# First layer: modulation blocks beside the heads, three instructions on three engines or one on VectorE

## The chip, the cores and the metric

The kernel runs on 1 core of one Trainium2 chip. The metric is the device time of one execution in microseconds (us), here the median of 3 runs. The engines are called as in the profile: PE (TensorE; PEld are its weight loads), DVE (VectorE), ACT (ScalarE), POOL (GpSimd), and SP, which does no arithmetic here and issues most of the transfers.

## The reference, cut to what matters

The network has two blocks on 512 tokens of width 1024; the change touches the first layer of the first block. Each layer of that block is modulated by vectors made from one conditioning vector `c`:

```python
c_act = jax.nn.silu(c)
mod = c_act @ w_ada[layer] + b_ada[layer]
shift, scale, gate = mod[:, :D], mod[:, D:2 * D], mod[:, 2 * D:]
h = _modulated_norm(x, norm_g[layer], shift, scale)
y = _gdn_mixer(h, ...)                       # first layer: 8 heads of a gated delta rule
x = x + gate[:, None, :] * y
```

The second layer needs its own `mod` and `mkv = c_act @ w_ada_kv + b_ada_kv`. In all these are 64 blocks of 128 outputs, and each is a product of a 128 x 1024 weight block with one vector of 1024, plus a bias.

## The kernel before, in words

A modulation block is made without PE. `ada` (lines 181 to 195) issues a 512 KB load of the weight block on SP's queue into a tile `ada` (line 187), and returns a function that does the arithmetic. With `off=False` that is one DVE instruction (line 189): it multiplies the tile with the vector `c_rep`, sums along the row and adds the bias, into one column of `mods`. With `off=True` it is three: the product on POOL (line 192), a copy with a running sum on ACT (line 193), and the addition of the bias, 128 x 1, on DVE (line 194).

The first 16 blocks (shift and scale of the first layer) are made at the start, on DVE, since nothing can be projected before them (`OFF` is empty). The other 48 are wanted later: the gate of the first layer in its output projection (line 346), the rest at the start of the second layer (lines 781 and 782). They stand in the list `late`, and are made beside the heads, from a pool of 2 buffers (line 394).

The eight heads come next. `project(h)` computes a head's four 128-column blocks of the input projection (`proj_T`): SP loads a weight block `wr`, ACT writes its rounded part `wh` (line 115), POOL in most cases the remainder `wl` (line 118), and PE runs three matmuls (lines 122 to 124). `conv` follows on ACT and DVE (lines 488 to 493). `gdn_head` has two long chains of small steps:
- the inverse of a triangular matrix in five levels (lines 651 to 670): POOL makes a masked copy `Lm` (line 653), PE and ACT alternate (lines 657 to 667), and DVE subtracts to give the next X (line 669);
- the scan over eight chunks (lines 686 to 702): PE (line 692), DVE (`u`, line 693), PE (line 696), DVE (state `S`, line 701), in turn.

At the end of a head DVE writes its output `oT` (line 717). A planner orders each engine's instructions ahead of time, so that one head's scan, the next head's inverse and the projection of the one after run side by side; each engine then works through its own list in order. What the planner may not do is put an instruction ahead of one it is tied to.

`aside(ins)` (line 513) is called six times in each head: behind the five X updates (line 669) and behind `oT` (line 717). Each call takes the oldest waiting block of the list `came`, issues its arithmetic with `tc.issue_after(ins.ins)`, and asks for the load of the next block (line 522). `issue_after` ties to `ins` only instructions on the engine of `ins`, which is DVE. In the kernel before, the DVE instruction of a block is the addition of the bias alone, so the product on POOL and the sum on ACT are free to run earlier. `came` starts with two blocks that are made with `off=False` (line 509), the 46 others have `off=True`. There are 48 calls, so all 48 blocks are taken by them, and the loop behind the heads (lines 537 to 542) finds nothing left.

After the heads, `residual` (line 561) projects `oT` with `w_out_a` in two parts: the first seven heads' share first, then the eighth's. Its input is split into `oH` on ACT (line 115) and `oL` on DVE (line 118).

Of the kernel before, what the change touches and what calls it, by code (L numbers as in the profile page):

```python
# [372 lines left out]
class Gdn(Net):  # L373
# [9 lines left out]
    def gdn(self):  # L383
# [5 lines left out]
        with ExitStack() as st:  # L389
# [4 lines left out]
            ap = st.enter_context(tc.tile_pool(name="g_ada", bufs=2))  # L394
# [101 lines left out]
            def silu_z(cb, p):  # L496
# [7 lines left out]
            late = [(w_, j0 + j, bias[:, j:j + 1], o[:, j:j + 1]) for w_, j0, n, bias, o in (  # L504
                (a["w_ada"][0], 16, 8, self.col("b_ada", 16, 8), self.mod0[:, 16:24]),
                (a["w_ada_kv"], 0, 16, self.col("b_ada_kv"), self.modk),
                (a["w_ada"][1], 0, 24, self.col("b_ada", 24, 24), self.mod1)) for j in range(n)]

            came = [self.ada(ap, *late.pop(0)) for _ in range(2)]
# [3 lines left out]
            def aside(ins):  # L513
                owed[0] += self.RATE
                if owed[0] < 1:
                    return
                owed[0] -= 1
                if came:
                    with tc.issue_after(ins.ins):
                        came.pop(0)()  # L520
                if late:
                    came.append(self.ada(ap, *late.pop(0), True))
            self.aside = aside

            def project(h):
# [12 lines left out]
            while late or came:  # L538
                if came:
                    came.pop(0)()  # L540
                if late:
                    came.append(self.ada(ap, *late.pop(0), len(late) % self.LV != 0))
            oH = hp.tile([P, KC, T], F32R, tag="hH", name="oH")
            oL = hp.tile([P, KC, T], F32R, tag="hL", name="oL")
            for k in range(KC):
# [1194 lines left out]
```

## Time and profile before

| what | us |
|---|---|
| median of 3 runs | 2809.49 |
| lowest and highest of them | 2806.31 and 2812.97 |
| the profiled execution, its own time | 2804.78 |
| its span, first to last instruction | 2803.0 |
| PE busy in the span | 2630.9 |
| POOL busy in the span | 1743.7 |
| DVE busy in the span | 1696.8 |
| ACT busy in the span | 1208.7 |

Times in the rows are us from the start of the span. The profiled execution lies 4.7 us below the median of the runs. Of the span, the first 110 us are the start and the first head's projection, 110 to 430 most of the work of the heads, and 430 to 510 the rest: the scan of the last two heads beside the output projection. A busy PE need not be PE at its peak, because matmuls are pipelined.

### The profile page before, as it was taken

Reading aid. Unit: us, or ns where it says so; the run is one execution under the profiler, and the core shown is the slowest. Engines: PE = TensorE matmul, PEld = TensorE weight load, DVE = VectorE, ACT = ScalarE, POOL = GpSimd, SP = SyncE. Lnnn points to the kernel's source line nnn. Section 1 sums busy time; section 2 is a strip of 40 time slices with the busy share of each in tenths; the row PEclk is TensorE's granted clock in tenths of the full one; section 3 lists DMA queues with packets and bytes.
Section 4 is the critical chain, followed back from the end, with each engine's and each line's share of the span. In section 5 each row is a group of like instructions: output and inputs, shape, how many; then the busy total and the mean of one; then the engine's idle time right before and its main releaser. Section 6 shows DMA issues by size and latency. Waiting matters only on the chain. (4 is left out here: it accounts for less than half of the span.)

```text
span 2803.0 us, 40405 instructions
## 1 busy us (share of the span) xinstructions
PE 2630.9 (94%) x14601; PEld 2246.9 (80%) x14601; DVE 1696.8 (61%) x3082; ACT 1208.7 (43%) x2505; POOL 1743.7 (62%) x1348
## 2 busy tenths in 40 slices
PE   6999998799997689999998999999999999999998
PEld 4887777697776577787777899999999977877776
DVE  7767663614446456222232597798776167678887
ACT  5676653636664344333333333344434333333332
POOL 4899873543232333444365368878788478887886
PEclk9999999899998799999999999999999999999999
DMA  6343331221011011222122378888888889999996
GB/s 241 106 142 122 116 103 32 77 92 61 29 42 50 31 55 52 78 73 76 65 72 97 124 262 298 311 292 314 312 296 312 280 286 333 344 331 334 334 325 227
DMA packets 206794, 499.35 MB, mean 178 GB/s; under 512 B 18305, under 2 KB 106625, under 8 KB 203521
## 3 DMA queue, kind: packets, MB, share of 16 engines
q1 hardware_dynamic: 167856, 359.19, 38.1%
q0 software_dynamic: 36864, 134.23, 13.4%
q10 hardware_dynamic: 1872, 3.33, 0.4%
q8 instruction: 115, 1.88, 0.3%
q14 instruction: 87, 0.70, 0.1%
HBM read 444.26 MB, written 52.43 MB: 177 GB/s over the span
## 5 line engine op out<-in xcount | busy, mean ns | idle before, releaser
L118 POOL TENSOR_TENSOR wl<-wr,wh 128x256 fp32r<-128x256 f32 (+2 forms) x513 | 425.3, 848 | 466.3 <-ACT wh L115 430.6
L118 POOL TENSOR_TENSOR upl<-upr,uph 128x1024 fp32r<-128x1024 f32 x128 | 311.9, 2437 | 96.5 <-ACT uph L115 95.5
L115 ACT ACTIVATE wh<-wr 128x256 fp32r<-128x256 f32 (+2 forms) x556 | 228.0, 445 | 326.4 <-PE pj L123 113.4
L122 PE MATMUL pj<-nH,downh 128*128 128x384 f32 x1024 | 352.5, 344 | 2.4 <-ACT w L1559 1.3
L124 PE MATMUL pj<-nH,downl 128*128 128x384 f32 x1024 | 348.9, 341 | 2.5 <-DVE downl L118 2.5
L123 PE MATMUL pj<-nL,downh 128*128 128x384 f32 x1024 | 348.9, 341 | 0.0
L118 POOL TENSOR_TENSOR downl<-downr,downh 128x1024 fp32r<-128x1024 f32 x96 | 238.2, 2483 | 131.0 <-ACT downh L115 129.8
L1604 PE MATMUL acc<-uph,wwh 128*128 128x512 f32 x768 | 301.6, 398 | 8.1 <-ACT wwh L115 8.1
L1604 PE MATMUL acc<-upl,wwh 128*128 128x512 f32 x768 | 305.2, 398 | 0.0
L115 ACT ACTIVATE downh<-downr 128x1024 fp32r<-128x1024 f32 x128 | 135.4, 1059 | 309.9 <-PE pj L123 191.6
L118 DVE TENSOR_TENSOR wwl<-wo,wwh 128x384 fp32r<-128x384 f32 x128 | 215.2, 1683 | 63.0 <-ACT wwh L115 59.8
L1604 PE MATMUL acc<-uph,wwl 128*128 128x512 f32 x768 | 232.2, 398 | 6.5 <-DVE wwl L118 6.4
L122 PE MATMUL pj<-hH,wh 128*128 128x512 f32 x544 | 224.5, 413 | 1.7 <-ACT mv L1290 0.7
L124 PE MATMUL pj<-hH,wl 128*128 128x512 f32 x544 | 221.2, 408 | 0.9 <-POOL wl L118 0.8
L123 PE MATMUL pj<-hL,wh 128*128 128x512 f32 x544 | 216.3, 398 | 0.0
L115 ACT ACTIVATE uph<-upr 128x1024 fp32r<-128x1024 f32 x128 | 134.8, 1053 | 174.9 <-POOL upl L118 122.8
L122 PEld LDWEIGHTS pj<-nH,downh 128*128 128x128 f32 x1024 | 193.0, 189 | 5.4 <-ACT downh L115 1.6
L124 PEld LDWEIGHTS pj<-nH,downl 128*128 128x128 f32 x1024 | 193.1, 189 | 3.7 <-DVE downl L118 3.5
L123 PEld LDWEIGHTS pj<-nL,downh 128*128 128x128 f32 x1024 | 193.1, 189 | 0.3
L1604 PEld LDWEIGHTS acc<-uph,wwh 128*128 128x128 f32 x768 | 144.7, 188 | 46.4 <-ACT wwh L115 11.6
L1604 PEld LDWEIGHTS acc<-uph,wwl 128*128 128x128 f32 x768 | 144.9, 189 | 43.8 <-DVE wwl L118 8.7
L1604 PEld LDWEIGHTS acc<-upl,wwh 128*128 128x128 f32 x768 | 145.1, 189 | 34.9
(627 smaller groups left out, 6549.8 us busy)
## 6 DMA issues: line engine op xcount, KB each, us to landing
downr<-in_peer_down_j SPq DMA_DIRECT2D x128, 512.0 KB, 4.8
upr<-in_peer_up_j SPq DMA_DIRECT2D x128, 512.0 KB, 5.7
wr<-in_w_in SPq DMA_DIRECT2D x50, 512.0 KB, 4.2
ada<-in_w_ada SPq DMA_DIRECT2D x48, 512.0 KB, 3.7
wait<-w SPq DMA_DIRECT2D x128, 192.0 KB, 4.9
wo<-wait SPq DMA_DIRECT2D x128, 192.0 KB, 4.9
G<-stage SPq DMA_DIRECT2D x24, 1024.0 KB, 7.3
Gt<-G SPq DMA_DIRECT2D x48, 512.0 KB, 7.9
```

The lines of the kernel that those rows point to most:

```text
L115: nc.scalar.activation(h, src, AF.Copy)
L118: return (eb or nc.vector).tensor_tensor(l, src, h.bitcast(F32), op=ALU.subtract)
L122: mm(out, lh, rh, start=start, stop=False)
L123: mm(out, lh, rl, start=False, stop=False)
L124: mm(out, ll, rh, start=False, stop=stop)
L1604: mm(po[z][b], lh[:, zs], rh[:, bs], start=False, stop=j == P - 1 and rh is uh and lh is l, skip_group_check=True)
```

## The change

Every block made beside the heads takes the form with one DVE instruction. The second edit makes the same choice in the loop behind the heads.

```diff
--- before.py
+++ after.py
@@ -519,7 +519,7 @@
                     with tc.issue_after(ins.ins):
                         came.pop(0)()
                 if late:
-                    came.append(self.ada(ap, *late.pop(0), True))
+                    came.append(self.ada(ap, *late.pop(0)))
             self.aside = aside
 
             def project(h):
@@ -539,7 +539,7 @@
                 if came:
                     came.pop(0)()
                 if late:
-                    came.append(self.ada(ap, *late.pop(0), len(late) % self.LV != 0))
+                    came.append(self.ada(ap, *late.pop(0)))
             oH = hp.tile([P, KC, T], F32R, tag="hH", name="oH")
             oL = hp.tile([P, KC, T], F32R, tag="hL", name="oL")
             for k in range(KC):
```

## Rows read from the trace of the kernel before

**Rows 1.** Busy time by stretch: start:end and length, then each engine, clock, DMA share, GB/s.
```profile
60.00:110.00 50.00, 49.44 (x258) 39.46 (x258) 40.80 (x70) 35.04 (x92) 33.91 (x39) 1.00 0.26 79
110.00:430.00 320.00, 299.07 (x1863) 254.17 (x1862) 221.32 (x401) 204.28 (x526) 286.05 (x241) 0.99 0.37 119
```
**Rows 2.** Groups by line, 110 to 430 us: busy us, mean ns, idle before.
```profile
L192 POOL TENSOR_TENSOR ada<-ada,c_rep 128x1024 f32<-128x1024 f32 x46 | 111.2, 2417 | 4.6 <-DMA ada<-in_w_ada 3.7 <-PE pj L124 0.5 <-DMA ada<-in_w_ada_kv 0.2
...
L193 ACT ACTIVATE ada<-ada 128x1024 f32<-128x1024 f32 x46 | 48.5, 1054 | 5.5 <-POOL ada L192 5.4
...
L194 DVE TENSOR_TENSOR mods<-mods,cols 128x1 f32<-128x1 f32 x40 | 31.8, 798 | 0.0
```
**Rows 3.** Tiles ada and mods: ns min/median/max, first and last start.
```profile
L192 POOL TENSOR_TENSOR ada<-ada,c_rep x46: 2336/2376/3083, 111.5 to 389.8; 128x1024 f32<-128x1024 f32 x46
...
L189 DVE CUSTOM_DVE_ANT_0 ada<-ada,c_rep,cols x18: 1268/1275/2414, 17.4 to 122.4; 128x1024 f32<-128x1024 f32 x18
...
L194 DVE TENSOR_TENSOR mods<-mods,cols x46: 141/369/4648, 137.2 to 499.4; 128x1 f32<-128x1 f32 x46
L189 DVE DVE_READ_ACCUMULATOR2_ANT mods<- x18: 72/76/82, 19.6 to 123.9; 128x1 f32 x18
...
L189 DVE CUSTOM_DVE_ANT_0 ada<-ada,c_rep,cols x1: 1534/1534/1534, 122.4 to 122.4; 128x1024 f32<-128x1024 f32 x1
```
**Rows 4.** Timeline near 233 us: start, us, instruction, idle before and its releaser.
```profile
232.83 2.39 POOL L192 TENSOR_TENSOR ada<-ada,c_rep 128x1024 f32<-128x1024 f32 x1
...
233.06 4.65 DVE L194 TENSOR_TENSOR mods<-mods,cols 128x1 f32<-128x1 f32 x1
...
238.37 0.33 PE L588 MATMUL n<-c_id,y 128*128 128x128 f32 x1 [0.85 <-DVE vb L637]
```
**Rows 5.** Timeline near 132, 292 and 382 us.
```profile
131.63 2.34 POOL L192 TENSOR_TENSOR ada<-ada,c_rep 128x1024 f32<-128x1024 f32 x1
...
131.94 2.05 DVE L594 TENSOR_TENSOR cols<-gcol,cols 128x8 f32<-128x8 f32 x1
...
134.04 0.65 PE L146 MATMUL n<-c_id,cols 128*128 128x128 f32 x4 [2.25 <-DVE cols L594]
...
291.30 3.06 DVE L711 TENSOR_TENSOR ss<-ss,cols 128x4 f32<-128x4 f32 x2
...
294.49 0.49 PE L569 MATMUL n<-rr,selr 128*128 128x512 f32 x1 [3.40 <-DVE rv_q L138]
...
382.18 2.24 DVE L594 TENSOR_TENSOR cols<-gcol,cols 128x8 f32<-128x8 f32 x1
...
385.94 0.80 PE L692 MATMUL s<-S,WQ 128*128 128x128 f32 x2 [2.57 <-DVE S L701]
```
**Rows 6.** What PE waited for, 110 to 430 us: total us, times, longest.
```profile
PE s L692 <- DVE S L701: 4.0, 4, 2.6
...
PE v L657 <- DVE Xv L669: 2.3, 5, 0.8
```
**Rows 7.** Timeline of DVE in the tail, 433 to 501 us.
```profile
433.21 0.35 DVE L701 SCALAR_TENSOR_TENSOR S<-S,gl,s 128x128 f32<-128x128 f32 x1 [0.63 <-PE s L696]
...
447.52 0.34 DVE L701 SCALAR_TENSOR_TENSOR S<-S,gl,s 128x128 f32<-128x128 f32 x1
...
500.18 0.69 DVE L118 TENSOR_TENSOR oL<-oT,oH 128x512 fp32r<-128x512 f32 x1 [0.63 <-ACT oH L115]
```
**Rows 8.** What SP waited for, 110 to 430 us: total us, times, longest.
```profile
SPq L187 <- ACT ada L193: 169.6, 34, 12.0
SPq L262 <- POOL wl L118: 50.4, 11, 16.5
```
**Rows 9.** The page: loads of the blocks (KB each, median us to landing).
```profile
ada<-in_w_ada SPq DMA_DIRECT2D x48, 512.0 KB, 3.7
```
**Rows 10.** Timeline of DVE near 150 us: three additions close together.
```profile
149.25 1.36 DVE L194 TENSOR_TENSOR mods<-mods,cols 128x1 f32<-128x1 f32 x2
...
151.13 0.70 DVE L194 TENSOR_TENSOR mods<-mods,cols 128x1 f32<-128x1 f32 x1
```

## The prediction

> **What bounds the kernel now.** The change lies in the stretch of the heads, so I looked at the busy times by stretch first [rows 1]. From 110 to 430 us PE is busy 299.1 of 320 us (93%), against 49.4 of 50 (99%) in the 50 us before, where no block is made beside the work. So PE sets the pace of the heads, and at most some 20 us of idle PE are to be had there. POOL is busy 286 us (89%) and DVE 221 (69%). Behind 430 us the scans of the last heads set the end. Next, the groups by line [rows 2]: the blocks take 111.2 us of POOL, its largest item, 48.5 of ACT and, for 40 additions of one column, 31.8 of DVE. An addition that can take 0.14 us takes 0.80 on average, and once 4.65 [rows 3]. The timeline says why [rows 4]: the long one starts 0.23 us behind a product of 2.39 us on POOL, and outlasts it. Others with both inputs in SBUF show the same: one of 128 x 8 takes 2.05 us beside a product that starts 0.31 us earlier and ends with it, and PE waits 2.25 us behind it [rows 5]. So the blocks cost PE little by their own work and something by what they hold up on DVE.
>
> **The change, part by part.** The sum is made on the profiled execution, 2804.78 us (span 2803.0), which is 4.7 us under the median of the runs.
>
> The second edit issues nothing: 48 calls take all 48 blocks, so the loop behind the heads is empty. Cost 0.
>
> POOL loses 46 products, 111.2 us, and ACT 46 copies, 48.5 us. Neither bounds the stretch, so that time as such is worth nothing; what counts is what waited for it. Four waits of PE can be read [rows 4, 5]. At 134.04 PE waited 2.25 us for an instruction that the product covers from 131.94 to 133.97: 2.0 back. At 385.94 it waited 2.57 us behind the same instruction of another head, stretched to 2.24: 2.1 back. At 294.49 it waited 3.40 us behind a pair stretched to 3.06; a pair can also stand behind POOL's other work, so I count two thirds, 2.2. At 238.37 the 4.65 us addition itself made 0.85. That is **-7.2 us**. The bounds: 0, if the planner puts other late work in those places, and -17.6, which is what 320 us would give up if PE were busy 99% as in the 50 us before (299.1/0.989 = 302.4).
>
> DVE gets 46 instructions of the long form. The trace has 18 at 1.27 us and up to 2.41 in the worst case; the only one beside the heads took 1.53, to which 0.08 for reading the sum comes [rows 3]. I take 1.61, because that one met the same neighbours. Of the 46, 40 lie before 430 us: 40 x (1.61 - 0.80) = 32.4 us more on DVE. What stands behind them is each time an X update or a state S of the other head. PE now waits 4.0 us for S and 2.3 for X [rows 6], 6.3 us beside 31.8 us of additions, or 0.20 of them. Passed on at that rate, 32.4 us make **+6.4 us**. The bounds are 0 and 32.4.
>
> The order changes too. Today the product runs as soon as POOL is free: the first starts at 111.5 us and its addition at 137.2, the last at 389.8 and its addition at 499.4 [rows 3]. Afterwards the whole work of a block is tied to the X update or `oT`. Six additions stand behind 430 us (46 less 40), and their whole blocks thus move into the tail, where POOL's part is long done. There the scan of the seventh head runs beside the last inverse, and four of its S stand right behind an addition [rows 7]: two with some 0.6 us of idle DVE between (0.63 at 433.21), two with none (447.52). With 1.35 in place of 0.15 us they come 0.6, 0.6, 1.2 and 1.2 us later, 3.6 us. PE reaches its next step late in some of these, so I take half, **+1.8 us**, bounds 0 and 3.6. The last block stands behind `oT` of the eighth head at 499.40, and delays `oL` at 500.18 [rows 7] by 1.2 - 0.6 = **+0.6 us**; nothing else is left for PE there.
>
> The transfers: no load is added, but the buffer of a block now comes free when its DVE instruction ends, and the load of the block after next waits for that. Product and sum had freed it earlier. Such a load lands 3.7 us after its issue [rows 9], so from one addition to the next but one 1.35 + 3.7 = 5.1 us are needed, and 46 additions over 362 us [rows 3] leave 15.7 on average. Close together they are near 150 us, three within 1.9 us [rows 10]. There DVE would stand 3.2 us, with X and S behind it; half of that is **+1.7 us**, bounds 0 and 3.2. SP, where the loads queue with the weights, is treated as a rival.
>
> Sum: -7.2 + 6.4 + 1.8 + 0.6 + 1.7 = +3.3 us, so 2808.1 on the profiled execution, **2812.8 us** on the median. A measurement of this kernel tells about 0.2% from no change, 5.6 us.
>
> The trace shows DVE held by POOL [rows 4, 5]; whether a DVE instruction also holds POOL no row here shows by itself. The Trainium skill, "SBUF — State Buffer", section "Who interferes with whom", says that a DVE instruction with two SBUF inputs and a GpSimd instruction that reads SBUF exclude each other, and that whoever issues first keeps the port for its whole length. By that rule the new instruction, whose tile and vector both lie in SBUF, holds up POOL in turn, and the time would be that of the third rival below.
>
> **The rivals.**
> 1. *Freed engines win (faster).* POOL falls to 175 of 320 us and ACT by a quarter, so masked copies, weight remainders and copies out of PSUM come when PE wants them, and the planner hides the DVE work behind projection matmuls. For: DVE has 99 us of idle time there, and POOL is close to full. Against: in the trace PE hardly waits for POOL itself. With PE at 99% and the tail as above: -17.6 + 2.4 = -15.2 us, 2794.3.
> 2. *DVE stands before a load (slower).* SP issues in order and stands for its buffers: 169.6 us before block loads and 50.4 before weight loads, there up to 16.5 us at a time [rows 8]. Today a late block load is POOL's matter. Afterwards the DVE instruction waits for it at the head of DVE's list, with X, S and the convolution behind it, so PE follows. It decides once SP holds a block load longer than the 15.7 - 5.1 = 10.6 us that an average pair leaves. If a quarter of 46, 12, wait 2 us each and PE loses all of it, that is +24; with 7.2 given back and 2.4 in the tail +19.2, or 2828.7.
> 3. *POOL is held (slower).* If each of 40 instructions holds POOL half its time, 0.68 us, that is 27 us, at 0.20 another +5.4: 2818.2. Against: POOL has 111 us more room.
> 4. *Nothing measurable depends on it*: all of it hides, 2809.5.
>
> **How the numbers follow.** Chances: forecast 0.42, freed engines 0.28, DVE before a load 0.22, POOL held 0.05, nothing 0.03. The forecast's own range is 2806 to 2820: its terms are sized by a rate taken from few waits, and the planner's new order adds a few us either way. Of its 0.42, 0.29 end within 5.6 us, 0.11 above, 0.02 below. Faster: 0.26 of freed engines and 0.02, 0.28. Slower: 0.11 + 0.21 + 0.05 = 0.37. The same: 0.35. The range over all cases is 2794 to 2831: it reaches to the two outer ones, and leaves out more gain than theirs and a longer standing of DVE.
>
> **What would show it.** In the profile after, POOL's busy time from 110 to 430 should be near 175 us and DVE's at most 254 (221 + 32.4), less what its other instructions no longer stand behind POOL. The 128 x 8 instruction should be back below 0.5 us on average, and PE's wait for it gone. PE's waits for S and X should rise from 6.3 to 10 to 15 us. If DVE has idle time that ends with a block's load, rival 2 is at work, and the number of such waits tells its price. If PE is busy above 97% in the heads, rival 1 has won and my rate of 0.20 is wrong. The forecast is wrong as a whole if the time moves without any of these, by the order of PE's work alone.

## The result and the profile after

The changed kernel takes 2829.95 us (median of 5 runs, 2826.38 to 2839.15) against 2809.49 (median of 5 runs of the kernel before in the same comparison): a ratio of 1.0068, interval 1.0047 to 1.009. It is slower by 0.7%, some 19 us, inside the range over all cases (2794 to 2831), but above the forecast's own range (2806 to 2820) and its point of 2812.8. The profiled execution took 2827.38 us, with a span of 2825.6.

Where the time goes shows at two instructions of DVE that both kernels have: line 781 is the first of the second layer, line 896 one of the first of the second block. First the kernel before, then the changed one, each from the timeline (start, us).

```profile
518.19 0.17 DVE L781 SCALAR_TENSOR_TENSOR sck<-mods,cols 128x8 f32<-128x8 f32 x1
...
903.00 0.25 DVE L896 TENSOR_SCALAR turns<-ang 128x32 f32<-128x32 f32 x2
```
```profile
528.23 0.17 DVE L781 SCALAR_TENSOR_TENSOR sck<-mods,cols 128x8 f32<-128x8 f32 x1
...
924.71 0.25 DVE L896 TENSOR_SCALAR turns<-ang 128x32 f32<-128x32 f32 x2
...
254.44 1.73 DVE L189 CUSTOM_DVE_ANT_0 ada<-ada,c_rep,cols 128x1024 f32<-128x1024 f32 x1 [2.19 <-DMA ada<-in_w_ada_kv]
...
259.83 0.57 PE L696 MATMUL s<-u,kd 64*128 64x128 f32 x2 [1.98 <-ACT ot L694]
...
259.94 1.68 DVE L189 CUSTOM_DVE_ANT_0 ada<-ada,c_rep,cols 128x1024 f32<-128x1024 f32 x1 [1.11 <-DMA ada<-in_w_ada_kv]
...
261.55 0.68 DVE L669 TENSOR_TENSOR Xv<-Xv,v 128x512 f32<-128x512 f32 x1
...
262.28 1.11 PE L657 MATMUL v<-c_id,Xv 128*128 128x128 f32 x4 [1.88 <-DVE Xv L669]
...
438.51 1.28 DVE L189 CUSTOM_DVE_ANT_0 ada<-ada,c_rep,cols 128x1024 f32<-128x1024 f32 x1 [1.38 <-DMA ada<-in_w_ada]
...
443.27 1.28 DVE L189 CUSTOM_DVE_ANT_0 ada<-ada,c_rep,cols 128x1024 f32<-128x1024 f32 x1 [0.67 <-DMA ada<-in_w_ada]
...
448.08 1.28 DVE L189 CUSTOM_DVE_ANT_0 ada<-ada,c_rep,cols 128x1024 f32<-128x1024 f32 x1 [1.11 <-DMA ada<-in_w_ada]
...
453.14 1.28 DVE L189 CUSTOM_DVE_ANT_0 ada<-ada,c_rep,cols 128x1024 f32<-128x1024 f32 x1 [1.91 <-DMA ada<-in_w_ada]
...
439.83 19.75 SPq L187 DMA_DIRECT2D ada<-in_w_ada  x5
```

In these two executions the first layer ends 10.0 us later, and the second, which the change doesn't touch, takes another 11.7 (396.5 in place of 384.8). How far one execution may stand for its kernel is taken up under the experiments. From line 896 to the end it is 1900.0 before (2803.0 - 903.0) and 1900.9 after. The other rows of the second fence show DVE standing before block loads, in series some 5 us apart, and at 262.28 what follows: the X update (261.55) stands behind a block that waited 1.11 us and took 1.68, and PE waits 1.88 us for it. The tile `ada` from 110 us on tells how often:

```profile
L189 DVE CUSTOM_DVE_ANT_0 ada<-ada,c_rep,cols x47: 1272/1284/2360, 120.9 to 509.4; 128x1024 f32<-128x1024 f32 x47
...
  DMA ada<-in_w_ada: 14.4, 15
  DMA ada<-in_w_ada_kv: 5.2, 5
```

That is 19.6 us in 20 waits. In all 20 the load that DVE waited for was issued 0.04 us after the block's instruction before it had ended, as at 439.83, the first of the five loads of that row (the instruction of 438.51 ends at 439.79), and landed 3.4 to 4.4 us later: it had stood for that instruction's buffer. In the kernel before the additions had no idle time in front of them [rows 2]. The next fence has busy times by stretch of the changed kernel, to be held against [rows 1], and the fence behind that has three stretches of the kernel before (columns as there).

```profile
60.00:110.00 50.00, 49.45 (x258) 39.51 (x257) 40.74 (x70) 34.94 (x92) 34.57 (x39) 1.00 0.29 84
110.00:430.00 320.00, 301.76 (x1840) 257.01 (x1838) 225.70 (x434) 156.81 (x431) 194.01 (x195) 0.97 0.34 105
110.00:528.00 418.00, 376.73 (x2189) 314.84 (x2187) 274.65 (x530) 191.67 (x523) 225.96 (x233) 0.95 0.32 101
...
255.00:260.00 5.00, 2.92 (x20) 2.31 (x19) 2.92 (x12) 3.08 (x15) 2.26 (x4) 1.00 0.50 175
260.00:265.00 5.00, 3.12 (x15) 2.84 (x16) 4.63 (x9) 1.37 (x3) 3.24 (x3) 0.51 0.34 105
265.00:270.00 5.00, 5.00 (x23) 4.87 (x23) 4.32 (x9) 1.98 (x5) 2.42 (x3) 0.50 0.30 105
...
700.00:850.00 150.00, 137.65 (x764) 105.43 (x765) 56.48 (x90) 87.60 (x187) 41.31 (x35) 0.94 0.10 33
```
Up to line 781 PE is idle 41.3 us after (418 - 376.7) and 37.3 before. The other 6.0 us are busier PE for the same work, which the clock can account for: 0.95 of 418 us against 0.97 of 408, which is some 21 and 12 us of full clock not granted. The rows from 255 to 270 us show such a place: PE is idle for 2.1 of the 5 us up to 260, and the granted clock, 1.00 until then, is 0.51 and 0.50 in the next two stretches, the lower level of 1.2 GHz. In the kernel before it stayed at 1.00 there:

```profile
110.00:518.00 408.00, 370.72 (x2192) 308.65 (x2190) 259.12 (x485) 238.29 (x616) 317.59 (x280) 0.97 0.32 105
255.00:270.00 15.00, 14.46 (x91) 12.34 (x90) 10.43 (x22) 9.44 (x20) 11.24 (x10) 1.00 0.32 116
...
700.00:850.00 150.00, 146.92 (x829) 110.24 (x828) 63.65 (x97) 92.67 (x197) 44.20 (x38) 1.00 0.11 33
```

Here waits of PE were paid twice, once as idle time and once in the clock behind them. Not every wait is: in the kernel before PE was idle for 3.5 of the 40 us from 230 to 270, and the granted clock stayed at 1.00.

What the freed engines should have given is there too. POOL is at 194.0 of 320 us and ACT at 156.8. The additions of 128 x 8 (line 594) are short again, and PE's waits for them are gone from the list of waits; those for X and S come to 5.7 us, no more than the 6.3 before [rows 6]:

```profile
PE v L657 <- DVE Xv L669: 4.0, 3, 1.9
PE s L696 <- ACT ot L694: 2.4, 2, 2.0
...
PE s L692 <- DVE S L701: 1.7, 2, 1.3
```

The groups by line, 110 to 430 us, with the last two columns as in [rows 2]:

```profile
L189 DVE CUSTOM_DVE_ANT_0 ada<-ada,c_rep,cols 128x1024 f32<-128x1024 f32 x38 | 56.0, 1473 | 13.2 <-DMA ada<-in_w_ada 7.9 <-DMA ada<-in_w_ada_kv 5.2
...
L594 DVE TENSOR_TENSOR cols<-gcol,cols 128x8 f32<-128x8 f32 x6 | 1.5, 251 | 0.1
```

So the trace names three places where time may have been lost: before loads, in the clock behind such waits, and in a layer that the change doesn't touch. What it gained can't be read from this trace; for that the parts had to be taken one at a time.

### The profile page after: what moved, and what is told of

It is laid out like the page before. It is cut to its first block, busy times and chain, and to the rows that moved or that the text cites. A ratio compares the mean times of both kernels' runs of the same rounds, so it can differ in the third digit from the quotient of the medians.

```text
span 2825.6 us, 40303 instructions
## 1 busy us (share of the span) xinstructions
PE 2638.9 (93%) x14601; PEld 2255.9 (80%) x14601; DVE 1705.4 (60%) x3128; ACT 1162.4 (41%) x2413; POOL 1650.3 (58%) x1302
## 3 DMA queue, kind: packets, MB, share of 16 engines
q8 instruction: 115, 1.88, 0.3%
## 5 line engine op out<-in xcount | busy, mean ns | idle before, releaser
L118 POOL TENSOR_TENSOR wl<-wr,wh 128x256 fp32r<-128x256 f32 (+2 forms) x513 | 434.5, 867 | 500.8 <-ACT wh L115 467.8
L122 PEld LDWEIGHTS pj<-nH,downh 128*128 128x128 f32 x1024 | 194.0, 189 | 5.4 <-ACT downh L115 1.6
L123 PEld LDWEIGHTS pj<-nL,downh 128*128 128x128 f32 x1024 | 194.0, 189 | 0.3
```

The costliest lines, as they stand in the source:

```text
L118: return (eb or nc.vector).tensor_tensor(l, src, h.bitcast(F32), op=ALU.subtract)
L122: mm(out, lh, rh, start=start, stop=False)
L123: mm(out, lh, rl, start=False, stop=False)
```

## The experiments

Where a text below says that an order is that of a kernel, each engine's list of instructions was tied, one behind the other, in the order that the planner had made for that kernel; nothing else is changed by it. "First layer ended" is the start of line 781 in the profiled execution. One plan gives times of a layer that differ by up to 10 us between executions, so verdicts go by the ratios; where I give them in us, a ratio is multiplied by 2810. The trace of the kernel before with another order in its second layer alone (second_as_after below) shows it: up to line 781 each engine's list is instruction for instruction that of the kernel before, and yet this layer ended at 528.5 in place of 518.2.

```profile
528.48 0.17 DVE L781 SCALAR_TENSOR_TENSOR sck<-mods,cols 128x8 f32<-128x8 f32 x1
...
926.79 0.26 DVE L896 TENSOR_SCALAR turns<-ang 128x32 f32<-128x32 f32 x2
```

The 10.0 us between the two traces above are thus no evidence by themselves that the first layer lost time.

### The second layer's order, there and back

The planner plans the whole block at once, and with the change 475 of the 2120 PE instructions of the second layer stand in another place of PE's list. The first kernel is the changed one with the second layer in the order of the kernel before; the second is the kernel before with the second layer in the order of the changed one.

```diff
+    n0 = len(tc.nc.cur_bb.bb.instructions)
     x = net.gdn()
     x = net.sb(x)
+    pinned(tc, n0, ORDERS)
```

> The kernel after, with one thing added: from the start of the second layer (line 765) to its end, PE, DVE, ACT and POOL are tied to the order that the planner made for the kernel before; the first layer is left to the planner. In the profile of the kernel after, the first instruction of the second layer (line 781) is 10.0 us late (528.2 against 518.2), and the last products of that layer (line 346) 22.1 us. Theory A, the planner's other order in the second layer costs the difference by itself: about 13 us less than the kernel after, 2816 to 2818, with line 781 still at 528. Theory B, the second layer is longer because of what the first leaves behind (clock, transfers): 2828 to 2831, the order making no difference.

> The kernel before, with one thing added: in the second layer the four engines are tied to the order that the planner made for the kernel after. No block is made otherwise than before. Theory A: 12 to 14 us slower than before, 2821 to 2824, with line 781 at 518 as before. Theory B: as before, 2807 to 2812.

Measured: 1.0042 (1.0026 to 1.0057) with the old order put back, and 1.0045 (1.0027 to 1.0063) with the new order alone, in a kernel whose blocks are made as before. The second is shown: a plan of a layer that nobody edited costs 12.6 us by the ratio, and its second layer took 398.3 us in the profile against 384.8. This is more than chance of one execution: the second layer took 384.8 to 393.2 us (388.7 on average) in the traces of all 12 kernels of this record that have the old order, and 396.5 and 398.3 in the two that have the new one, some 9 us more. The rows of 700 to 850 us are alike in both kernels that have this order (the changed kernel's stands above, this one follows), with PE 10 us more idle and the clock at 0.94 in place of 1.00:

```profile
700.00:850.00 150.00, 137.04 (x761) 104.76 (x762) 56.78 (x89) 87.58 (x187) 41.74 (x36) 0.94 0.11 36
```

The first is weaker: 1.0068 and 1.0042 have intervals that overlap. The old order saves some 7 us of the 19, and the other 12 stay (1.0042 is clear of 1), in the first layer, which is all that is left of the change. The expectation for line 781 was missed in both traces, by 5 us (533.1) and by 10 (528.5).

### What the work of POOL and ACT costs, and what long DVE instructions cost

Both kernels keep all orders of the kernel before, in both layers. The first cuts the product and the sum of a late block to one column, and so leaves out the late modulation vectors; the second also puts a minimum over 1024 resident columns (1.21 us, no load read) in the place of each addition, and leaves out the same.

```diff
-            nc.gpsimd.tensor_tensor(raw, raw, self.c_rep, op=ALU.mult)
-            nc.scalar.activation(raw, raw, AF.Copy, accum_out=out)
+            nc.gpsimd.tensor_tensor(raw[:, :1], raw[:, :1], self.c_rep[:, :1], op=ALU.mult)
+            nc.scalar.activation(raw[:, :1], raw[:, :1], AF.Copy, accum_out=out)
```

In the second kernel also:

```diff
-            nc.vector.tensor_tensor(out, out, bias, op=ALU.add)
+            nc.vector.tensor_reduce(out, self.c_rep, axis=AX.X, op=ALU.min)
```

> The kernel before, with the product on POOL and the sum on ACT cut to one column, so that the modulation vectors of the late blocks are left out; all instructions stay, and all four engines are tied to the order of the kernel before through both layers. So only the work that the blocks put on POOL and ACT goes. My term for that was -7.2 us: line 781 at 511, 2802. If freed engines are worth all of PE's idle time, -17.6: line 781 at 501, 2792. If nothing was held up by them: 518 and 2809.

> As the kernel with the work cut to one column, and in the place of each addition on DVE a reduction over 1024 columns of a vector that is always there (the late modulation vectors are left out). The orders of all four engines are those of the kernel before, and no DVE instruction waits for a load. My terms for the longer DVE instruction were +6.4 and +2.4 us: line 781 at 519 to 520, 2810 to 2812, 8 to 9 us above the kernel with the work cut. If the length on DVE makes the whole loss of the first layer: line 781 at 528 or later, 2819. If it hides: 511 and 2802, no difference from the kernel with the work cut; then the loss of the first layer comes from the order or from the waits for loads.

Measured: 0.9907 (0.9888 to 0.9927) without the work, first layer ended at 495.4; 0.9945 (0.9926 to 0.9965) with the minimum, ended at 506.4. So the work on POOL and ACT costs 26 us by the ratio (22.7 in the profile), and 46 DVE instructions of 1.21 us in the place of additions cost 10.7 (11.0). With the orders held, the trade would have been a gain of 15, if the block's real instruction cost no more than this minimum. How much of the 26 comes from POOL and ACT themselves and how much from DVE, whose additions are no longer held and fall from 0.71 to 0.29 us on average, no run tells apart.

Where the 22.7 us had been is read from the busy times of the first kernel:

```profile
110.00:430.00 320.00, 311.82 (x1986) 267.73 (x1984) 184.33 (x427) 175.09 (x546) 189.92 (x246) 1.00 0.39 121
...
110.00:495.00 385.00, 363.33 (x2196) 305.92 (x2194) 213.49 (x487) 200.67 (x616) 216.24 (x280) 0.98 0.36 111
```

Up to line 781 PE is idle 21.7 us, against 37.3 in the kernel before: 15.6 less. It is busy 363.3 against 370.7 for the same matmuls: 7.4 less, of which the clock can make some 4.5 (7.7 us not granted, against 12.2).

### The new order of the first layer, without load waits

Two kernels with the changed kernel's order in the first layer, and that of the kernel before in the second. The late block's instruction reads no load: in one it is the minimum over resident columns, in the other a 128 x 1 addition. Both leave out the late modulation vectors.

```diff
-                    came.append(self.ada(ap, *late.pop(0)))
+                    came.append(self.ada(ap, *late.pop(0), late=True))
...
+        if late:
+            return lambda: nc.vector.tensor_reduce(out, self.c_rep, axis=AX.X, op=ALU.min)
```

In the lighter one the last line is:

```diff
+            return lambda: nc.vector.tensor_tensor(out, self.c_rep[:, :1], bias, op=ALU.add)
```

> The changed kernel with its own order of the first layer and, in the second, the order of the kernel before. The instruction of each late block is a minimum over the 1024 resident columns of the gate vector (about 1.2 us, no load read), so that VectorE waits for no load of a block; the loads are still made. Left out: the late modulation vectors. Beside it stands work_shrunk_long (order of the kernel before, the same minimum): 2795.3 us, first layer ended at 506. Theory (VectorE's waits for the block loads are the loss): 2795 to 2803, first layer ended at 506 to 514, some 22 to 30 us below second_as_before (2825.2). Rival (the new order of the first layer is itself the loss, the waits are covered): 2815 to 2825, first layer ended at 522 to 533.

> As order_long, but the instruction of a late block is a 128x1 addition that reads no load, so that no engine has work for the late blocks. Left out: the late modulation vectors. Beside it stands work_shrunk (order of the kernel before): 2786.0 us, first layer ended at 495. Theory (the order costs nothing by itself): 2782 to 2790, first layer ended at 492 to 500. Rival (the new order costs by itself): 2800 to 2808, first layer ended at 508 to 518. Either way the step from here to order_long is the price of 1.2 us on VectorE 48 times without a load wait: 9 to 11 us.

Measured: 1.0004 (0.9983 to 1.0025) and 0.998 (0.9963 to 0.9998), first layer ended at 518.3 and 511.2. By these, the new order costs 20 us with light instructions (0.998 less 0.9907), against the theory. But the pair isn't what it was meant to be: nothing reads the landing buffers, so they come free at once, and the last late load was issued at 219 and 217 us in place of 459 in the changed kernel. From 110 to 300 us the DMA engines were busy 0.53 and 0.55 of the time, against 0.44 in work_shrunk (the row is order_light's):

```profile
110.00:300.00 190.00, 185.47 (x1084) 158.23 (x1083) 107.22 (x220) 93.64 (x243) 108.07 (x121) 0.98 0.55 179
```

Order and early loads are mixed here, and I draw no price from them. The step between the two, for the long instruction without a load, is 0.0024 or 6.7 us, with intervals that overlap. Whether the changed kernel's order of the first layer costs time by itself stays open.

### Four landing buffers, and the same instruction in the old order

`aside` ties every sixth block to `oT` of a head, and its load is made long before. It holds one of the two buffers until the head ends, and the five blocks tied to the next head's X updates share the other: 3.7 us of load [rows 9] and 1.35 of work make the 5 us between the rows at 438 to 453 us. If that is right, more buffers, or blocks that aren't tied, take the waits away. The first kernel is the changed one with four buffers (its first layer planned anew, the second in the order of the kernel before). The second has the orders of the kernel before everywhere, the blocks' instructions in the places of the additions, dealt out by their number and not tied.

```diff
-            ap = st.enter_context(tc.tile_pool(name="g_ada", bufs=2))
+            ap = st.enter_context(tc.tile_pool(name="g_ada", bufs=4))
```
```diff
-                    with tc.issue_after(ins.ins):
-                        came.pop(0)()
+                    came.pop(0)()
```

> The changed kernel with four landing buffers for the blocks in place of two, the second layer in the order of the kernel before. Theory (VectorE waits for loads because the block tied to a head's end holds one of two buffers): its waits for block loads fall from 20 us to under 5 and the time from 2825 to 2808 to 2815, first layer ended at 512 to 520. Rival (order at fault): waits gone, and still 2820 to 2828.

> The one VectorE instruction for each late block, but every engine's order in both layers that of the kernel before: a block's instruction stands where an addition stood, the blocks dealt to these places by their number, not tied to an instruction of the heads; two landing buffers. Theory (freed engines are worth some 23 us, the long VectorE instructions cost 9 to 11, no order and few load waits to pay): 2795 to 2802, first layer ended at 504 to 512, faster than both kernels. Rival (the load waits come with two buffers in any order): 2812 to 2825, with over 12 us of VectorE idle before block loads.

Measured: four_buffers 0.9999 (0.9981 to 1.0018), before_order 0.999 (0.9971 to 1.0009), first layer ended at 527.0 (in an execution of 2822.2, where the median is 2812.0) and at 517.8. The waits, in the tile `ada` of each from 110 us on:

```profile
L189 DVE CUSTOM_DVE_ANT_0 ada<-ada,c_rep,cols x47: 1270/1280/2146, 122.5 to 495.1; 128x1024 f32<-128x1024 f32 x47
...
  DMA ada<-in_w_ada: 0.9, 1
```
```profile
L189 DVE CUSTOM_DVE_ANT_0 ada<-ada,c_rep,cols x47: 1268/1280/2359, 122.1 to 498.6; 128x1024 f32<-128x1024 f32 x47
...
  DMA ada<-in_w_ada: 2.1, 1
```

Two buffers with the tie: 20 waits. Four with the tie: one. Two without the tie: one. The mechanism of the waits is shown. Its price is not shown by itself: from second_as_before to four_buffers it is 0.0043 or 12 us (the intervals don't touch), but four_buffers has a new plan of the first layer as well, and a kernel planned anew can lose 47 us for reasons that stay open (before_four below). In the traces, up to line 781, PE is idle 42.3 us in second_as_before and 39.1 in four_buffers, whose traced execution lies 10 us above its median. before_order missed its expectation of 2795 to 2802 by 6 us: it has neither the waits nor a new order, and stands 12.6 us above work_shrunk_long all the same. Something in the instruction itself was left.

### Two operands of 1024 columns

The minimum reads one operand, the real instruction two, and it reads the landed block; it also writes 1024 columns where the minimum writes one. The next two kernels are before_order with one of these changed: a minimum over the landed block, or the gate vector multiplied by itself with no load made. Both leave out the late modulation vectors, the second the late loads too.

```diff
-            return lambda: nc.vector.tensor_tensor_reduce(raw, raw, self.c_rep, 1.0, bias, ALU.mult, ALU.add, out)
+            return lambda: nc.vector.tensor_reduce(out, raw, axis=AX.X, op=ALU.min)
```
```diff
-        nc.sync.dma_start(raw, w[j])
-            return lambda: nc.vector.tensor_tensor_reduce(raw, raw, self.c_rep, 1.0, bias, ALU.mult, ALU.add, out)
+            return lambda: nc.vector.tensor_tensor_reduce(raw, self.c_rep, self.c_rep, 0.001, bias, ALU.mult, ALU.add, out)
```

> As before_order (2807.9 us: every engine's order that of the kernel before, two landing buffers), but a late block's instruction is a minimum over the landed block: it waits for the load and reads it, but takes one operand of 1024 columns in place of two. Left out: the late modulation vectors. Beside it stands work_shrunk_long (the same minimum over resident columns, 2795.3). Theory (an instruction with two operands of 1024 columns and GpSimd hinder each other: GpSimd's low part of a weight half took 865 ns in before_order against 779 in work_shrunk_long): 2795 to 2800, first layer ended at 506 to 511, the low part of a weight half back near 780 ns. Rival (VectorE reads landed blocks, and so waits for loads and frees buffers late): 2804 to 2810, first layer ended at 515 to 520.

> As before_order, but a late block is not loaded; its instruction multiplies the gate vector by itself (two operands of 1024 columns, resident, product written to the landing buffer). Left out: the late loads and the late modulation vectors. Theory (two operands against GpSimd): 2803 to 2809, first layer ended at 513 to 519, the low part of a weight half near 865 ns as in before_order. Rival (the loads): 2793 to 2799, first layer ended at 503 to 509.

Measured: one_input 0.9954 (0.9936 to 0.9972), first layer ended at 506.6; no_loads 0.9972 (0.9955 to 0.999), ended at 514.1. Waiting for the load and reading it costs 2.5 us over work_shrunk_long, and the second operand, with the wide write, another 10.1. By way of no_loads it is 7.6 for the operand and 5.1 for the load. POOL's groups from 110 to 450 us show what goes with it, in one_input, no_loads, before_order and the changed kernel in turn, with the block's instruction on DVE for one_input and before_order (`wl` is line 118, the masked copy line 653 in the kernel before):

```profile
L118 POOL TENSOR_TENSOR wl<-wr,wh 128x256 fp32r<-128x256 f32 x87 | 68.2, 787 | 61.9 <-ACT wh L115 59.7 <-PE s L693 1.0 <-PE pj L124 0.9
L654 POOL TENSOR_TENSOR Lmv<-Ls,c_lv 128x512 f32<-128x512 f32 x38 | 48.7, 1283 | 27.8 <-PE v L663 25.4 <-PE s L697 2.4
...
L189 DVE TENSOR_REDUCE mods<-ada 128x1 f32<-128x1024 f32 x45 | 54.4, 1211 | 2.0 <-DMA ada<-in_w_ada 2.0
```
```profile
L118 POOL TENSOR_TENSOR wl<-wr,wh 128x256 fp32r<-128x256 f32 x87 | 74.4, 860 | 58.2 <-ACT wh L115 57.4 <-PE pj L124 0.6
L655 POOL TENSOR_TENSOR Lmv<-Ls,c_lv 128x512 f32<-128x512 f32 x38 | 52.5, 1382 | 27.7 <-PE v L664 26.0 <-PE s L698 1.7
```
```profile
L118 POOL TENSOR_TENSOR wl<-wr,wh 128x256 fp32r<-128x256 f32 x87 | 74.9, 865 | 61.6 <-ACT wh L115 60.8 <-PE pj L124 0.6
L652 POOL TENSOR_TENSOR Lmv<-Ls,c_lv 128x512 f32<-128x512 f32 x38 | 52.6, 1385 | 27.4 <-PE v L661 25.7 <-PE s L695 1.7
...
L189 DVE CUSTOM_DVE_ANT_0 ada<-ada,c_rep,cols 128x1024 f32<-128x1024 f32 x45 | 64.3, 1429 | 2.1 <-DMA ada<-in_w_ada 2.1
```
```profile
L118 POOL TENSOR_TENSOR wl<-wr,wh 128x256 fp32r<-128x256 f32 x87 | 80.0, 930 | 42.7 <-ACT wh L115 35.3 <-PE pj L123 6.0 <-PE pj L124 1.2
L653 POOL TENSOR_TENSOR Lmv<-Ls,c_lv 128x512 f32<-128x512 f32 x38 | 53.8, 1417 | 37.9 <-PE v L662 37.9
```

POOL's remainder takes 787 ns on average in the kernel whose blocks take one operand, 860 and 865 in those with two, whether the operands were loaded or not, and 930 in the changed kernel. That DVE holds POOL shows when the same groups are parted by whether they ran beside a block's instruction: in before_order the 21 remainders that overlap one took 1149 ns on average and the 66 others 775, and the masked copies 1671 (10) and 1282 (28). In one_input the remainders took 812 (18) and 781 (69), the copies 1283 and 1282. DVE is held as well: its instruction has a median of 1280 ns but takes 1429 on average, which with 80 ns for reading the sum is 0.30 us more than the minimum, 13.7 us over 46 of them; at the 0.25 worked out below that makes 3.4 of the 10 us.

How the rest reaches PE is not shown: PE's own waits for POOL from 110 to 450 us come to 1.0 us in before_order and 0.9 in one_input. Nor does a run part the second operand from the wide write; the additions of the kernel before, which write one column and were held by POOL [rows 4], speak for the operand. That the two intervals, 0.9936 to 0.9972 and before_order's 0.9971 to 1.0009, just touch is the weak point of the price; that both kernels with two operands show POOL at 860 to 865 is the strong one of the mechanism.

### Two attempts at a better kernel

Half the late blocks on one DVE instruction and half on three engines, with four buffers; and the kernel before with four buffers. Both have the second layer in the order of the kernel before.

```diff
-                    came.append(self.ada(ap, *late.pop(0)))
+                    came.append(self.ada(ap, *late.pop(0), len(late) % 2 == 0))
```

> 23 of the late blocks by the one VectorE instruction, 23 in between by three engines as before, with four landing buffers; the first layer in the program's own order, the second in that of the kernel before. Theory (what GpSimd's share costs grows faster than its share, and so does what VectorE's costs): 2796 to 2804, faster than both kernels. Rival (each block costs its own, wherever it goes): between the kernel before (2810) and four_buffers (2812), 2807 to 2814.

> The kernel before with four landing buffers in place of two, all late blocks by three engines, the second layer in its own order. Theory (in the kernel before the block loads are covered: GpSimd waited 3.9 us for them in 8 waits): 2806 to 2813, no change that can be told. Rival (two buffers hold up the kernel before as well): 2796 to 2804, and what four_buffers gained is no gain of the change's.

Measured: 1.0067 (1.0041 to 1.0093) and 1.0169 (1.014 to 1.0197): both slower, outside every expectation. In the second, with room for four loads, the products run from 57.5 to 286.9 us in place of 111.5 to 389.8 [rows 3]. From 110 to 300 us POOL is busy 172 of 190 us, PE is idle for 31, and the clock is 0.88. The last fence has the kernel before in the same stretch:

```profile
L192 POOL TENSOR_TENSOR ada<-ada,c_rep x46: 2341/2378/3932, 57.5 to 286.9; 128x1024 f32<-128x1024 f32 x46
```
```profile
110.00:300.00 190.00, 158.75 (x856) 131.78 (x855) 120.03 (x175) 109.81 (x261) 172.08 (x127) 0.88 0.41 132
```
```profile
110.00:300.00 190.00, 176.05 (x1088) 149.50 (x1087) 138.46 (x231) 123.53 (x313) 181.55 (x148) 1.00 0.39 127
```

It isn't how densely POOL's work stands: the kernel before has POOL busier there, 181.6 us, with PE idle for 14 and the clock at 1.00. What differs besides is the planner's new order of the first layer, and where the 47 us come from no run shows. Why half_each is slow is open too: POOL waited 26.5 us for its loads there in 18 waits, but no run takes that wait away. No version beat both kernels by more than the measurement tells; before_order is level with the kernel before (0.999) and faster than the changed one.

## Why the prediction was right and wrong

The range over all cases held by 1 us, and by luck: its upper end is the sum of the second rival, whose parts were wrong (below). The forecast's own range and the point did not hold: +3.3 us was summed, 19 were measured. The single steps of the way, from ratios times 2810:

| step | from, to | us |
|---|---|---|
| work of POOL and ACT gone | the kernel before, work_shrunk | -26.1 |
| 1.21 us on DVE 46 times | work_shrunk_long | +10.7 |
| the landed block is waited for and read | one_input | +2.5 |
| a second operand of 1024 columns, and the wide write | before_order | +10.1 |
| the program's own order, four buffers | four_buffers | +2.5 |
| two buffers, with the tie and another plan | second_as_before | +12.1 |
| the second layer's new order | the changed kernel | +7.3 |
| sum | | +19.1 |

Each step has an uncertainty of some 5 to 8 us, so the two of 2.5 are not told from zero, and the last one stands only together with second_as_after. The sum is the measured 1.0068 by the way the table is made, and no check of it.

**"That is -7.2 us", with -17.6 as the outer bound, failed.** It was -26, beyond the bound. I counted four waits that I could read in the timeline, and bounded the rest by PE's idle time up to 430 us at 99% busy. Both leave out what work_shrunk showed: PE idle 15.6 us less up to line 781, behind 430 us too, and busy 7.4 us less for the same matmuls, of which the clock can make 4.5. That a busy PE need not be PE at its peak stood beside the profile, and I passed over it.

**"Passed on at that rate, 32.4 us make +6.4", with 2.4 in the tail, held for the length alone and failed for the instruction.** Together these are 8.8, and the minimum of 1.21 us cost 10.7. The additions took 0.29 us on average in work_shrunk, so the minimum adds 0.92 us 46 times, 42 us of DVE, and the rate was 0.25 where I had 0.20. There is luck in that: the 2.57 us wait at 385.94, which the first term gives back, is also the longest of the waits behind the 0.20, which without it is 0.12. The real instruction, with its load and its second operand, cost 23.3 us in the same order (work_shrunk to before_order), more than twice the term. I expected PE's waits for S and X to rise from 6.3 to 10 to 15 us, and they stayed at 5.7. The minimum alone did raise them, from 2.8 us in work_shrunk to 6.3 in work_shrunk_long, a third of what it cost.

**"The transfers", at +1.7, failed.** I took the distance from one addition to the next but one, as if two buffers alternated. I did not see that every sixth block, tied to `oT`, keeps one of them until its head ends; then five blocks have one buffer, and need 5 us each, where the X updates stand closer (13.2 of the 19.6 us lie before 430 us). With the new plan of the first layer, which no run parts from it, this cost 14.6 us (before_order to second_as_before). This is the second rival's mechanism, DVE standing before a load at the head of its list, and 20 waits of 1 us took the place of the 12 of 2 us assumed there. The rival's 2828.7 lies 1 us from the result, but not by its working: its price of 24 us for the waits was too high even against those 14.6, and it did not have the second operand, the second layer's order, or the size of the gain. Nor was its point of decision right: it wasn't SP's queue that held the loads, but the buffers.

**The third rival had 0.05 and 5.4 us, and was right in kind.** POOL's remainder takes 1149 ns where it overlaps a block's instruction in before_order and 775 elsewhere, and 812 and 781 with the minimum of one_input: POOL is held by DVE. The Trainium skill, "SBUF — State Buffer", "Who interferes with whom", says that a DVE instruction with two SBUF inputs and a GpSimd instruction reading SBUF shut each other out, and that `tensor_reduce` never does so on this chip; the runs agree with both (work_shrunk_long's 1.21 us minima leave POOL's remainder at 779 ns). I argued it away with "POOL has 111 us more room". before_order stands 10 us above one_input all the same, though what of that came by way of POOL is not shown.

**The first rival, freed engines, was right in its gain and wrong in its sum.** The gain was larger than it claimed, 26.1 us against 17.6, and it left out what DVE costs POOL, the waits for buffers and the second layer.

**No step had the second layer.** The prediction said it would be wrong if the time moved by the order of PE's work alone. A part of it did: second_as_after shows 12.6 us from an order alone, and the table has 7.3 for it. Of the other signs, DVE's 225.7 us (at most 254) and the 128 x 8 addition at 251 ns came as forecast; POOL stood at 194 in place of 175; the longer remainders and copies make some 14 of these 19 us (87 at 927 in place of 805 ns, 36 at 1398 in place of 1298).

## What to carry to other kernels

Taking work off an engine that "hides" can be worth more than the waits one can name: shrink that work to one column with every order held, and measure, before trusting a sum of waits. Count who holds each buffer and until when, not how far apart its uses are on average; one use tied to a late event takes a buffer out of the ring. Where a planner orders the whole program, hold its order while testing a change, since a new plan of untouched work is itself worth as much as the change. And before two traces are compared stage by stage, see how far two executions of one plan lie apart: here 10 us in one layer, as much as the difference to be explained.

## What was not expected of the hardware

The granted clock decides more than I thought, in small pieces. In the 12 runs of four_buffers the fastest, 2802.4 us, had a mean granted clock of 0.976 and the slowest, 2822.2, one of 0.971; 0.005 of 2810 is 14 of these 20 us. The same plan thus gives times that differ by 0.7%. A place at 1.2 GHz stands in the changed kernel from 260 to 270 us above: it begins behind one wait of PE, and a second falls into it.
